# Kernel study: gate matmuls of sample tokens in pairs, state-space outputs of eight heads in one go, and the decays' clamp on ScalarE

## The chip, the cores and the metric

The kernel runs on one NeuronCore of one Trainium2 chip. The metric is the device time of one execution in microseconds. A core has a matrix engine (TensorE, PE in the profile), a vector engine (VectorE, DVE), a scalar engine for activation functions (ScalarE, ACT), a general engine (GpSimd, POOL) and an engine that only issues transfers (SyncE, SP). Each engine has its own list of instructions, in an order set when the program is built; semaphores make one wait for another. Transfers between HBM and SBUF go through queues, here those of SP, ACT and POOL. TensorE's results lie in PSUM, of which the kernel uses eight banks.

## What is computed

One decoder layer for 256 prompt tokens and 8 x 8 sample tokens, 320 columns in all. One input projection feeds two mixers, and their outputs, side by side, go through one output projection; then comes a feed-forward network with a short convolution. The change touches the two mixers. The first gates inside chunks of 128 tokens (16 heads), the second is a state-space scan (SSD, 32 heads in 4 groups):

```python
# chunk_spatial_gate
v = layer_norm(jax.nn.gelu(a_v), ln_g, ln_b)
w = jnp.where(mask[None], w_s[:, :q, :q], 0)
s = jnp.einsum("hts,bnshd->bnthd", w, vp) + b_s
out = jax.nn.gelu(a_u) * s
# ssd_scan
da_cs = jnp.cumsum(dt * a)                       # in a chunk
seg = da_cs[:, :, :, None] - da_cs[:, :, None, :]
decay = jnp.exp(jnp.where(mask, seg, -jnp.inf))
cb = jnp.einsum("bctgn,bcsgn->bctsg", cc, bc)
y_diag = jnp.einsum("bctsgr,bcsgrp->bctgrp", cb[..., None] * decay, xdt)
```

In the kernel the exponent of a decay is clamped at zero before Exp, so that the entries the mask drops stay finite; the mask itself is in `cb`. Weights are float32; each is split into a rounded high part and a low part, and a product of weights and activations is three matmuls (high x high, high x low, low x high).

## The kernel before

**Weights.** `slab` (line 116) loads 128 x 1024 weights through SP's queue, casts them on ScalarE (`whi`, line 128) and subtracts on VectorE (`wlo`, line 130). Each of the three buffers `wraw`, `whi`, `wlo` has three copies. `accumulate` (139) issues the three matmuls, lines 141 to 143, of 320 columns. `project` (166) multiplies into four banks of the pool `mm` and hands each to an evacuation; `chunk_out` (222) multiplies one chunk of mixed activations by `w_out` or `ffn_w_down`. The other four banks, pool `ms`, serve everything small through `misc` (57).

**Order.** The program is unrolled. The framework orders each engine's instructions when the program is built, by priority (by default the place in the program, with `tc.high_priority` and `first` moving things ahead) and by when it estimates that they are ready. `tc.issue_after(x)` puts what is traced inside it, on the engine of `x` only, behind `x` in that engine's order. Background work is written as generators in the list `bg`; `tick` (154) advances the first of them by one step, once or `rate` times behind each slab, and `finish` runs one to its end.

**Gate.** After the v projection `turned` (593) transposes v to tokens on partitions, `vt`, with the prompt's two chunks in columns 0 and 1 of its second axis and the 64 sample tokens on partitions 0 to 63 of column 2; partitions 64 to 127 there are zeroed. `layer_norm` (651) normalizes it in four quarters of 512 features, with rows of gains and offsets that POOL's queue loads, two quarters at once and then one by one as the buffers come free. `gate_mix` (689) does four heads: per head two 128 x 128 matmuls for the prompt (line 710) and one for the samples (711), whose right side `wS` holds the 8 x 8 causal weights as a block diagonal, 64 columns wide. VectorE adds the bias, multiplies by u and splits the result.

**SSD.** `steps` (465) makes the step sizes and the sums of `dt * a`: `nda` holds their negatives with tokens on partitions, and `dacs_d`, in HBM, the sums with tokens along a row. `ssd(g)` (769) is one generator for each group of eight heads: it transposes x, loads states, makes `cb`, and then, for each head, `decays` (876). A pair of heads has one tile `cs` with its rows of sums, broadcast to all partitions by `load_sums` (782; three buffers). For each head `decays` adds the column of `nda` and takes the minimum with 0 (line 889, three pieces: two of 128 columns and one of 64), exponentiates (891) and multiplies by `cb` (893). For a pair it makes `cpx`, the decayed C for the carried state (two buffers). `products(j)` (896) is the matmuls of a pair of heads into one small bank (line 904, float32, half the array's columns a head) and the evacuation on VectorE (914). The generator makes four heads' decays with a step behind each, then two products, then the same again, and loads the fourth pair's sums between.

**Stages.** The SSD generators run behind the slabs of the projections and of `chunk_out` for `w_out`, from about 425 to 730 us. From 810 the post-norm is applied by `x1_ready` (1031) and the FFN begins; `renewals` (1147) holds, at its head, the adds and stores of three prompt states (1158, 1159).

## Time and profile before

| | |
|---|---|
| time, three runs | 1773.45, 1774.44 and 1777.11 us, median 1774.44 |
| the profiled execution | 1774.31 us, its span 1772.6 us |
| granted TensorE clock over the span | 0.999 |
| busiest line of the chain | 141 to 143 on `ps`, 20.7% to 20.9% of the span each |
| float32 matmuls of line 904 | 256 records, 22.0 us busy |
| float32 matmuls of lines 710 and 711 | 64 and 32 records, 15.7 us busy |
| relus and minima | line 889, 96 instructions on VectorE |

The page's first part gives each engine's busy time; the span runs from the first instruction to the last. A matmul in float32 shows as two records, and a matmul's record is its latency: they overlap, so the step from one start to the next, or the pieces of the chain of waits, give what one costs. The chain follows back from the last instruction what released each step. A group's row gives its count, its busy time, the mean of one, then the idle time of the engine in front of it and what ended that.

### The profile page before, as it was taken

Reading aid. Unit: us, or ns where it says so; the run is one execution under the profiler, and the core shown is the slowest. Engines: PE = TensorE matmul, PEld = TensorE weight load, DVE = VectorE, ACT = ScalarE, POOL = GpSimd, SP = SyncE. Lnnn points to the kernel's source line nnn. Section 1 sums busy time; section 2 is a strip of 40 time slices with the busy share of each in tenths; the row PEclk is TensorE's granted clock in tenths of the full one; section 3 lists DMA queues with packets and bytes.
Section 4 is the critical chain, followed back from the end, with each engine's and each line's share of the span. In section 5 each row is a group of like instructions: output and inputs, shape, how many; then the busy total and the mean of one; then the engine's idle time right before and its main releaser. Section 6 shows DMA issues by size and latency. Waiting matters only on the chain.

```text
span 1772.6 us, 31221 instructions
## 1 busy us (share of the span) xinstructions
PE 1765.2 (100%) x12223; PEld 1740.8 (98%) x12223; DVE 1183.2 (67%) x2052; ACT 800.8 (45%) x1111; POOL 281.5 (16%) x593
## 2 busy tenths in 40 slices
PE   9999999999999999999999999999999999999998
PEld 9999999999999999998999999999999999999998
DVE  7448854657877777678866666666666565656475
ACT  7344545333545454445645434343434343433335
POOL 2003210000111111012322212021101010101004
PEclk9999999999999999999999999999999999999999
DMA  7455554445664644444555656566554444444443
GB/s 251 138 167 167 191 156 149 155 152 183 226 208 150 206 154 151 154 164 155 169 190 191 210 177 201 188 196 200 185 187 153 148 155 147 157 148 152 153 148 107
DMA packets 228562, 303.04 MB, mean 171 GB/s; under 512 B 19488, under 2 KB 150656, under 8 KB 228224
## 3 DMA queue, kind: packets, MB, share of 16 engines
q1 hardware_dynamic: 216560, 281.27, 49.6%
q10 hardware_dynamic: 10448, 15.57, 2.4%
q0 software_dynamic: 1408, 4.23, 0.8%
q8 instruction: 96, 1.57, 0.4%
q14 instruction: 50, 0.41, 0.1%
HBM read 283.44 MB, written 17.58 MB: 170 GB/s over the span
## 4 chain that ended last, share of the span: by engine, by line
PE 98%; DVE 1%; DMA 0%; issue 0%; SPq 0%; POOL 0%; ACT 0%; DVEq 0%; ACTq 0%
PE ps L141 21%; PE ps L143 21%; PE ps L142 21%; PE pd L141 10%; PE pd L142 10%; PE pd L143 10%; PE y_ps L904 1%; PE sg L710 0%; PE yo_ps L853 0%; PE up_ps L1198 0%; PE tsum L282 0%; PE xt_ps L382 0%; PE vt_ps L599 0%; DMA vf<-in_w_in 0%; PE s_ps L835 0%; PE x1p L1233 0%
## 5 line engine op out<-in xcount | busy, mean ns | idle before, releaser
L130 DVE TENSOR_TENSOR wlo<-wraw,whi 128x1024 fp32r<-128x1024 f32 x470 | 581.4, 1237 | 383.2 <-ACT whi L128 380.6
L128 ACT CAST whi<-wraw 128x1024 fp32r<-128x1024 f32 x470 | 492.2, 1048 | 703.0 <-PE ps L142 411.5
L141 PE MATMUL ps<-h_hi,whi 128*128 128x320 f32 x2528 | 782.7, 310 | 0.0
L142 PE MATMUL ps<-h_lo,whi 128*128 128x320 f32 x2528 | 780.2, 309 | 1.4 <-DVE h_lo L371 1.4
L143 PE MATMUL ps<-h_hi,wlo 128*128 128x320 f32 x2528 | 779.7, 309 | 0.2 <-DVE wlo L130 0.2
L142 PEld LDWEIGHTS ps<-h_lo,whi 128*128 128x128 f32 x2528 | 475.0, 188 | 2.8 <-DVE h_lo L371 1.9
L141 PEld LDWEIGHTS ps<-h_hi,whi 128*128 128x128 f32 x2528 | 474.7, 188 | 3.1 <-issue 1.6
L143 PEld LDWEIGHTS ps<-h_hi,wlo 128*128 128x128 f32 x2528 | 474.6, 188 | 0.9 <-DVE wlo L130 0.7
L141 PE MATMUL pd<-fhi,whi 128*128 128x320 f32 x704 | 217.3, 309 | 0.0
L143 PE MATMUL pd<-fhi,wlo 128*128 128x320 f32 x704 | 217.3, 309 | 0.0
L142 PE MATMUL pd<-flo,whi 128*128 128x320 f32 x704 | 217.3, 309 | 0.0
L141 PE MATMUL pd<-ohi,whi 128*128 128x320 f32 x448 | 138.7, 310 | 0.0
L142 PE MATMUL pd<-olo,whi 128*128 128x320 f32 x448 | 138.6, 310 | 0.0
L143 PE MATMUL pd<-ohi,wlo 128*128 128x320 f32 x448 | 138.3, 309 | 0.0
L142 PEld LDWEIGHTS pd<-flo,whi 128*128 128x128 f32 x704 | 132.1, 188 | 0.7
L143 PEld LDWEIGHTS pd<-fhi,wlo 128*128 128x128 f32 x704 | 132.1, 188 | 0.0
L141 PEld LDWEIGHTS pd<-fhi,whi 128*128 128x128 f32 x704 | 132.1, 188 | 0.0
L234 DVE TENSOR_TENSOR acc_ffn<-acc_ffn,pd 128x320 f32<-128x320 f32 x160 | 77.3, 483 | 33.2 <-PE pd L143 32.0
L1091 POOL COPY ptf<-pad 128x2 f32<-128x2 f32 x88 | 22.6, 258 | 405.6 <-DVE pad L1079 405.0
L141 PEld LDWEIGHTS pd<-ohi,whi 128*128 128x128 f32 x448 | 84.1, 188 | 0.9 <-issue 0.4
L142 PEld LDWEIGHTS pd<-olo,whi 128*128 128x128 f32 x448 | 84.1, 188 | 0.7 <-issue 0.4
L143 PEld LDWEIGHTS pd<-ohi,wlo 128*128 128x128 f32 x448 | 84.1, 188 | 0.2 <-issue 0.2
(303 smaller groups left out, 1582.6 us busy)
## 6 DMA issues: line engine op xcount, KB each, us to landing
wraw<-in_ffn_w_up SPq DMA_DIRECT2D x176, 512.0 KB, 3.5
wraw<-in_w_in SPq DMA_DIRECT2D x142, 512.0 KB, 3.5
wraw<-in_ffn_w_down SPq DMA_DIRECT2D x88, 512.0 KB, 3.3
wraw<-in_w_out SPq DMA_DIRECT2D x64, 512.0 KB, 3.3
st<-in_state_ssm SPq DMA_DIRECT2D x64, 256.0 KB, 4.6
out_ssm_state_sample<-st ACTq DMA_DIRECT2D x32, 256.0 KB, 2.6
cs<-dacs_d SPq DMA_DIRECT2D x16, 320.0 KB, 4.5
xr<-in_xT SPq DMA_DIRECT2D x4, 640.0 KB, 4.6
```

Of the source, the lines that this page charges most:

```text
L128: act.copy(hi[:, :m], raw[:, :m])
L130: dve.tensor_tensor(out=lo[:, :m], in0=raw[:, :m], in1=hi[:, :m].bitcast(F32), op=ALU.subtract)
L141: pe.matmul(ps, whi, xhi, start=first, stop=False)
L142: pe.matmul(ps, whi, xlo, start=False, stop=False)
L143: newest[0] = pe.matmul(ps, wlo, xhi, start=False, stop=last).ins
L234: dve.tensor_tensor(out=acc[:, nb, :], in0=acc[:, nb, :], in1=ps[:, :NT], op=ALU.add)
L904: pe.matmul(ps[64 * i:64 * i + 64, cols], w(hl), x(hl, m, cpx), tile_position=(0, 64 * i), **flags)
L1091: pool.tensor_copy(ptf[:, k, :], pad[:, 256:258])
```

## The change

- **Paired samples.** The normalized sample rows of the odd heads are copied, quarter by quarter, by four transfers on POOL's queue to partitions 64 to 127 of `vt`'s third column. `wS` becomes two block diagonals side by side for each pair of heads, one on the lower and one on the upper partitions, zero elsewhere, and one matmul of 128 columns makes both heads' samples. `w8` is loaded for 128 partitions.
- **Rows.** The third and fourth quarters' gains and offsets are loaded at once, into buffers of the tag `vf`.
- **Eight heads.** `ssd` makes all eight decays, a step behind each, then a step, then four products. All four `load_sums` come at once; `cs` and `cpx` have four buffers.
- **Clamp.** `sda` holds the sums themselves (copied, not negated). ScalarE takes relu(-m + sda) in three pieces, the column as bias, and then Exp with scale -1; the three VectorE instructions of line 889 go.
- **Order.** The Exp of `cpx` is issued behind the last Silu that stood in the program when the generator began. The prompt states' add and store are traced inside an edge behind the last split of `x1_ready`, which is on ScalarE.
- **Memory.** The descriptor memory of POOL's queue is 1024 bytes a partition instead of 4096.

```diff
...
+        silus = []
+
         def conv_proj(c0, k0, out, soon=0):
...
                 act.activation(o[:, :NP], t[:, :NP], AF.Silu)
-                act.activation(o[:, NP:NT].rearrange("p (b t) -> p b t", b=NB),
-                               t[:, 259:347].rearrange("p (b r) -> p b r", r=11)[:, :, 0:TS], AF.Silu)
+                made = act.activation(o[:, NP:NT].rearrange("p (b t) -> p b t", b=NB),
+                                      t[:, 259:347].rearrange("p (b r) -> p b r", r=11)[:, :, 0:TS], AF.Silu)
+                silus.append(made.ins)
             project(w_in, c0, evac, quiet=4)
...
         dt = op.tile([P, 5, NH], F32, name="dt")
-        nda = op.tile([P, 3, NH], F32, name="nda")
+        sda = op.tile([P, 3, NH], F32, name="sda")
         dec = op.tile([P, 5, NH], F32, name="dec")
...
-            pool.memset(nda[:, 2], 3e38)
+            pool.memset(sda[:, 2], -3e38)
             ps = misc("cs_ps")
...
                 pe.matmul(ps[64 * r:64 * r + 64, 2 * NH:3 * NH], upper_s[:NS], da[:NS, 2], start=True, stop=True, tile_position=(0, 64 * r))
-            dve.tensor_scalar(out=nda[:, 0:2].rearrange("p c h -> p (c h)"), in0=ps[:, :2 * NH], scalar1=-1.0, scalar2=None,
-                              op0=ALU.mult)
-
-            n4 = nda[:, 2].rearrange("p (g r i) -> p g r i", g=4, r=2)
+            dve.tensor_copy(sda[:, 0:2].rearrange("p c h -> p (c h)"), ps[:, :2 * NH])
+
+            n4 = sda[:, 2].rearrange("p (g r i) -> p g r i", g=4, r=2)
             p4 = ps[:, 2 * NH:3 * NH].rearrange("p (g r i) -> p g r i", g=4, r=2)
...
                 x_at, s_at = slice(64 - 64 * r, P - 64 * r), slice(64 * r, 64 * r + 64)
-                dve.tensor_scalar(out=n4[x_at, :, r], in0=p4[x_at, :, r], scalar1=-1.0, scalar2=None, op0=ALU.mult)
+                dve.tensor_copy(n4[x_at, :, r], p4[x_at, :, r])
                 act.activation(ed[s_at], p4[s_at, :, r], AF.Exp)
...
-            wS = gp.tile([P, 4, NB, TS], F32, name="wS")
-            pool.memset(wS[NS:], 0.0)
+            wS = gp.tile([P, 2, 2, NB, TS], F32, name="wS")
+            pool.memset(wS, 0.0)
...
             def turned(g, vf):
-                if g == 0:
-                    pool.memset(vt[NS:, 2], 0.0)
                 for c, (o, n) in enumerate(TOK):
...
-                def load(q):
-                    cs = slice(512 * q, 512 * q + 512)
-                    for name, src in (("lg", gate_ln_g), ("lb", gate_ln_b)):
-                        rows.append(gp.tile([P, 512], F32, tag=name, name=name, bufs=2))
-                        with tc.issue_after(after_v[0]):
-                            pool.dma_start(rows[-1], src[0:1, cs].broadcast_to([P, 512]))
-                load(0)
-                load(1)
+                def load(q, src, row):
+                    with tc.issue_after(after_v[0]):
+                        pool.dma_start(row, src[0:1, 512 * q:512 * q + 512].broadcast_to([P, 512]))
+                    return row
+                both = [("lg", gate_ln_g), ("lb", gate_ln_b)]
+                for q in range(2):
+                    rows.append([load(q, src, gp.tile([P, 512], F32, tag=name, name=name, bufs=2)) for name, src in both])
+                late = [gp.tile([P, 4, NT], F32, tag="vf", name=name, bufs=2).rearrange("p k n -> p (k n)") for name, _ in both]
+                for q in range(2):
+                    rows.append([load(2 + q, src, row[:, 512 * q:512 * q + 512]) for row, (_, src) in zip(late, both)])
                 yield
...
                         v = vt[:n, c, 512 * q:512 * q + 512]
-                        dve.scalar_tensor_tensor(out=v, in0=v, scalar=mv[:n, c, 0:1], in1=rows[2 * q][:n], op0=ALU.subtract, op1=ALU.mult)
-                        dve.scalar_tensor_tensor(out=v, in0=v, scalar=lr[:n, c:c + 1], in1=rows[2 * q + 1][:n], op0=ALU.mult, op1=ALU.add)
-                        if c == 2 and q < 2:
-                            load(q + 2)
+                        dve.scalar_tensor_tensor(out=v, in0=v, scalar=mv[:n, c, 0:1], in1=rows[q][0][:n], op0=ALU.subtract, op1=ALU.mult)
+                        dve.scalar_tensor_tensor(out=v, in0=v, scalar=lr[:n, c:c + 1], in1=rows[q][1][:n], op0=ALU.mult, op1=ALU.add)
+                        if c == 2:
+                            two = vt[:, 2, 512 * q:512 * q + 512].rearrange("p (i r f) -> p i r f", r=2, f=P)
+                            pool.dma_start(two[NS:, :, 0], two[:NS, :, 1])
                         yield
...
                 wT = gp.tile([P, 4, P], F32, tag="wT", name="wT", bufs=1)
-                w8 = gp.tile([NS, 4, TS], F32, tag="w8", name="w8", bufs=1)
+                w8 = gp.tile([P, 4, TS], F32, tag="w8", name="w8", bufs=1)
                 bs = gp.tile([P, 4, P], F32, tag="bs", name="bs", bufs=1)
...
                     for j in range(4):
-                        dve.tensor_tensor(out=wS[:NS, j], in0=w8[:, j].unsqueeze(1).to_broadcast([NS, NB, TS]),
-                                          in1=upper_s[:NS].rearrange("p (b t) -> p b t", b=NB), op=ALU.mult)
+                        rs = slice(NS * (j % 2), NS * (j % 2) + NS)
+                        dve.tensor_tensor(out=wS[rs, j // 2, j % 2], in0=w8[rs, j].unsqueeze(1).to_broadcast([NS, NB, TS]),
+                                          in1=upper_s[rs].rearrange("p (b t) -> p b t", b=NB), op=ALU.mult)
                 yield
...
                         pe.matmul(ps[:, P * c:P * c + P], vt[:, c, fs], wT[:, j, :], start=True, stop=True)
-                    pe.matmul(ps[:, NP:NT], vt[:, 2, fs], wS[:, j].rearrange("p b t -> p (b t)"), start=True, stop=True)
+                    if j % 2 == 0:
+                        pe.matmul(ps[:, NP:NP + 2 * NS], vt[:, 2, fs], wS[:, j // 2].rearrange("p r b t -> p (r b t)"), start=True, stop=True)
+                        of_two = ps[:, NP:NP + 2 * NS].rearrange("p (r b t) -> p r b t", r=2, b=NB)
                     s = tp.tile([P, NT], F32, tag="ev", name="s", bufs=2)
...
                     dve.tensor_tensor(out=s[:, NP:].rearrange("p (b t) -> p b t", b=NB),
-                                      in0=ps[:, NP:NT].rearrange("p (b t) -> p b t", b=NB),
+                                      in0=of_two[:, j % 2],
                                       in1=bs[:, j, :TS].unsqueeze(1).to_broadcast([P, NB, TS]), op=ALU.add)
...
-                xs = x_of[g]
+                xs, last_silu = x_of[g], silus[-1]
                 h0 = 8 * g
...
-                    cs = sd.tile([P, 2, NT], F32, tag="cs", name="cs", bufs=3)
+                    cs = sd.tile([P, 2, NT], F32, tag="cs", name="cs", bufs=4)
                     o = NS * (j // 2)
...
                 yield from repeat(None, 5)
-                sums_of = {j: load_sums(j) for j in range(3)}
+                sums_of = {j: load_sums(j) for j in range(4)}
                 yield
...
                         cs = sums_of.pop(j)
-                        cpx = sd.tile([P, 2, P], F32, tag="cpx", name="cpx", bufs=2)
-                        act.activation(cpx, cs[:, :, at[1][0]:at[1][0] + P], AF.Exp)
+                        cpx = sd.tile([P, 2, P], F32, tag="cpx", name="cpx", bufs=4)
+                        with tc.issue_after(last_silu):
+                            act.activation(cpx, cs[:, :, at[1][0]:at[1][0] + P], AF.Exp)
                         pool.tensor_tensor(out=cpx, in0=cpx, in1=cT[:, g, P:2 * P].unsqueeze(1).to_broadcast([P, 2, P]),
...
                     for c, (o, n) in enumerate(at):
-                        dve.tensor_scalar(out=m[:, o:o + n], in0=m[:, o:o + n], scalar1=nda[:, c, h0 + hl:h0 + hl + 1],
-                                          scalar2=0.0, op0=ALU.add, op1=ALU.min)
-                    act.activation(m, m, AF.Exp)
+                        act.activation(m[:, o:o + n], m[:, o:o + n], AF.Relu, bias=sda[:, c, h0 + hl:h0 + hl + 1], scale=-1.0)
+                    act.activation(m, m, AF.Exp, scale=-1.0)
                     o = NS * (hl // 4)
...
                 x1d = decayed(1, 1)
-                for j in range(0, 4, 2):
-                    for hl in range(2 * j, 2 * j + 4):
-                        decays(hl)
-                        yield
+                for hl in range(8):
+                    decays(hl)
                     yield
+                yield
+                for j in range(4):
                     products(j)
-                    products(j + 1)
-                    if j == 0:
-                        sums_of[3] = load_sums(3)
                 pool.tensor_tensor(out=by_head(s1), in0=by_head(s1),
...
                 yield
-                pool.tensor_tensor(out=s1, in0=s1, in1=x1d, op=ALU.add)
-                act.dma_start(o_ssm_p[g], s1)
+                with tc.issue_after(whole[KD - 1]):
+                    pool.tensor_tensor(out=s1, in0=s1, in1=x1d, op=ALU.add)
+                    act.dma_start(o_ssm_p[g], s1)
...
         "gate_wT": w_s.transpose(2, 0, 1),
-        "gate_w8": np.concatenate([w8] * NB),
+        "gate_w8": np.concatenate([w8] * (P // TS)),
         "gate_b_s": a["gate_b_s"], "ssm_dt_bias": a["ssm_dt_bias"], "ssm_a_log": a["ssm_a_log"],
...
-    nc = _bacc.Bacc("TRN2", target_bir_lowering=False, num_devices=1, dynamic_dma_scratch_size=4096)
+    nc = _bacc.Bacc("TRN2", target_bir_lowering=False, num_devices=1, dynamic_dma_scratch_size=1024)
     arrays = laid_out({k: _np.asarray(v) for k, v in inputs.items()})
...
```

## The prediction

> **What bounds the kernel now.** I read the page first: span, busy shares, the chain of waits.
>
> ```profile
> span 1772.6 us, 31221 instructions
> PE 1765.2 (100%) x12223; PEld 1740.8 (98%) x12223; DVE 1183.2 (67%) x2052; ACT 800.8 (45%) x1111; POOL 281.5 (16%) x593
> PE 98%; DVE 1%; DMA 0%; issue 0%; SPq 0%; POOL 0%; ACT 0%; DVEq 0%; ACTq 0%
> ```
>
> TensorE is busy for 1765.2 of 1772.6 us and makes 98% of the chain that ended last. The other four engines have room over the whole span, but a share over the span says nothing of a stage, so I took the stages in which the diff does something (start:end, length, then busy time of PE, PEld, DVE, ACT, POOL, the granted clock, DMA share, GB/s), then TensorE's own waits (us in all, times, longest) and, in the timeline of ScalarE, the last Silu of the fourth group and two weight casts that follow each other.
>
> ```profile
> 145.00:260.00 115.00, 115.00 (x791) 114.02 (x789) 85.10 (x162) 59.51 (x85) 30.92 (x54) 1.00 0.56 174
> 515.00:730.00 215.00, 214.76 (x1620) 206.73 (x1613) 160.69 (x323) 107.94 (x157) 24.11 (x43) 1.00 0.52 168
> 676.00:705.00 29.00, 28.76 (x246) 26.13 (x246) 22.39 (x44) 12.16 (x18) 4.69 (x4) 1.00 0.45 141
> 810.00:822.00 12.00, 10.63 (x51) 7.32 (x50) 9.44 (x20) 6.04 (x11) 4.00 (x3) 0.86 0.30 108
> PE ps L142 <- DVE h_lo L371: 1.4, 2, 1.2
> 676.21 0.25 ACT L427 ACTIVATE xs<-cv 128x64 f32<-128x64 f32 x1
> ...
> 687.85 1.05 ACT L128 CAST whi<-wraw 128x1024 fp32r<-128x1024 f32 x1 [2.47 <-PE pd L142]
> 691.37 1.05 ACT L128 CAST whi<-wraw 128x1024 fp32r<-128x1024 f32 x1 [2.47 <-PE pd L142]
> ```
>
> In the layer-norm stage (145 to 260) and in the SSD stage (from 425; its last 215 us are the second row) TensorE has no idle time worth the name: 0.24 us in 330. The casts are 691.37 - 687.85 = 3.52 us apart, one weight slab; a slab is 8 blocks of three matmuls, so a weight matmul takes TensorE 0.147. An edit there can shorten the run only where it takes work off TensorE, and can lengthen it only where it makes TensorE wait. VectorE, at 75% of that second row, and ScalarE, at 50%, are not what ends last there. The one place with a wait that the diff comes near is 810:822, where TensorE stands 1.4 us for the first parts of the FFN's input.
>
> **The paired samples (lines 710 and 711).** The chain of waits around one group's gate matmuls, TensorE from one weight slab to the next; xN counts records, two for a float32 matmul:
>
> ```profile
> 259.52 0.44 PE sg L710 x4
> 259.96 0.17 PE sg L711 x2
> 260.13 0.50 PE sg L710 x4
> ...
> 262.14 0.20 PE ps L141
> ...
> 434.15 0.87 PE xt_ps L382 x8
> ```
>
> Four heads take 262.14 - 259.52 = 2.62 us. A record with 128 columns costs 0.44 / 4 = 0.11; one with 64 columns costs 0.17 / 2 = 0.085, not half, and the next four then cost 0.50 instead of 0.44, so a 64-column matmul hides the next weight load badly. After the change each pair of heads has one 128-column matmul where it had two of 64: four heads have 16 + 4 = 20 records of 128 columns. The transposes (eight in 0.87, 0.109 each) say that such a record holds its price in a row. 20 x 0.11 = 2.20, so 0.42 is saved for each of four groups: **1.7 us**, all on the path. From below: if the paired matmul cost as much as the two it replaces (0.34), only the 0.06 behind two of them would go, 0.1 in a group, 0.4 in all. I take 1.7, since the records of the same shape stand right beside it.
>
> ```profile
> L669 POOL DMA_DIRECT2D lb<-in_gate_ln_b x4 | 2.2, 541 | 0.4 <-DVE vt L677 0.4
> ...
> L130 DVE TENSOR_TENSOR wlo<-wraw,whi 128x1024 fp32r<-128x1024 f32 x470 | 581.4, 1237 | 383.2 <-ACT whi L128 380.6
> ...
> L914 DVE SCALAR_TENSOR_TENSOR xs<-xs,prm,y_ps 128x320 f32<-128x320 f32 x16 | 8.6, 542 | 7.9 <-PE y_ps L904 7.9
> ```
>
> What this edit needs lies off the path: four more transfers on POOL's queue (odd heads' rows copied to partitions 64 to 127, each issued behind the last normalization step of its quarter), the same small VectorE products on other partitions, a larger w8. On POOL's queue the conv stage's padding copies stand behind those transfers, VectorE's evacuation behind the copies, and TensorE's next use of those banks behind the evacuation; the row 145:260 shows 84 us of idle POOL and 30 of idle VectorE in that stretch. I cost it at nothing; without that cover the four issues, at 0.541 each as line 669's, would come to 2.2 us. (The other two rows of this view of groups are for the banks, below.) The same holds for the layer-norm rows, now loaded at once into buffers of the v projections: the loads no longer stand behind VectorE's steps, and the steps they feed end long before the matmuls at 259.52.
>
> **The y products in one go (line 904).** Chain rows, first group and then the second:
>
> ```profile
> 478.25 1.69 PE y_ps L904 x32
> 479.94 0.35 PE pd L141
> ...
> 559.27 0.36 PE y_ps L904 x2
> 559.63 0.34 PE pd L142
> ...
> 560.41 1.69 PE y_ps L904 x27
> ...
> 576.22 0.36 PE y_ps L904 x2
> ...
> 577.08 0.91 PE y_ps L904 x13
> ...
> 581.27 0.36 PE y_ps L904 x2
> ...
> 582.00 0.92 PE y_ps L904 x13
> ```
>
> A block of two products takes 1.69, and the first weight matmul behind it 0.35 where one takes 0.147: each return from float32 to the split weights costs 0.20. One block a group instead of two saves one return in the first, third and fourth group: 0.6 us. The second group is cut up today: its pieces add up to 0.36 + 1.69 + 0.36 + 0.91 + 0.36 + 0.92 = 4.60 where two blocks would be 3.38, and weight matmuls stand behind four of the pieces, the first at 0.34, where one block has one return. Whole, it saves 1.22 + 0.6. So the term lies between 0.6, if the new order is cut up as much as the old, and 2.4. The order of each engine is fixed when the program is built, and no row shows the new one. All eight heads' decays now stand well ahead of the first product, with buffers for all of them (cs 4, cpx 4), which speaks for whole blocks; ScalarE has more to do before them, which speaks for pieces. I take the middle, **1.5 us**.
>
> **The clamp moved to ScalarE (lines 889 and 891).** Groups by line and form, count, then busy time and mean ns:
>
> ```profile
> L891 ACT ACTIVATE cs<-cs 128x320 f32<-128x320 f32 x32 | 14.3, 466 | 20.3 <-DVE cs L889 20.1
> L367 ACT CAST ohi<-s 128x320 fp32r<-128x320 f32 x16 | 7.3, 459 | 16.5 <-DVE s L719 16.4
> L882 ACT ACTIVATE cpx<-cs 128x256 f32<-128x256 f32 x16 | 6.7, 416 | 11.4 <-DMA cs<-dacs_d 11.1 <-PE y_ps L904 0.2
> L370 ACT ACTIVATE ohi<-xs,prm 128x320 fp32r<-128x320 f32 x12 | 6.3, 556 | 0.0
> L427 ACT ACTIVATE xs<-cv 128x64 f32<-128x64 f32 x16 | 3.9, 242 | 0.0
> L891 ACT ACT_TABLE_LOAD x3 | 3.8, 1283 | 0.1
> ...
> L889 DVE TENSOR_SCALAR cs<-cs,nda 128x128 f32<-128x128 f32 x64 | 19.7, 335 | 6.0 <-DMA cs<-dacs_d 5.2 <-ACT cpx L882 0.7
> L889 DVE TENSOR_SCALAR cs<-cs,nda 128x64 f32<-128x64 f32 x32 | 8.4, 264 | 0.0
> ```
>
> VectorE is rid of 19.7 + 8.4 = 28.1 us. ScalarE gets 64 relus of 128 columns and 32 of 64, which no row shows. Without a per-partition operand 64 columns take 242 and 256 take 416, so 128 lie at 300; such an operand costs 556 - 459 = 97. That gives 397 and 339: 25.4 + 10.8 = 36.2 us, or 27.0 if the bias were free. I take 36.2, since the bias here is a column as the scale of line 370 is.
>
> A head then costs ScalarE 2 x 0.397 + 0.339 + 0.466 = 1.60 us, a group of eight with four of line 882 14.5 us. Two heads beside one slab's cast: 3.20 + 0.42 + 1.05 = 4.67, where a slab takes TensorE 3.52. So ScalarE falls 1.15 us behind with each slab of decays, 4.6 over four. What hides it: the casts of the slabs stand ahead by priority and wait 2.47 us for a free buffer before each, with three buffers (two slabs, 7.0 us, less 1.05 for the cast and 1.24 for the subtraction behind it); and the decays need not run beside the slabs of their ticks. They wait only for their sums, a buffer and the last Silu. The tightest group is the fourth, whose last Silu starts at 676.21: in 676:705 ScalarE has 12.16 us now, decays of its first heads among them; with all of these kept, 12.16 + 14.5 = 26.7 of 29. It fits, so I cost it at **nothing**. From above, with that cover gone, the products wait 4.6 us in each group, 18.4 in all. From below there is no gain, since VectorE is off the path.
>
> A table load takes 1.283 us; if relu and Exp did not share a table, each head would add two. The Trainium skill (ScalarE: Activation LUTs, "Table sets: the hidden batching unit") says that relu is in every set; by it no load is added, and otherwise the 64 loads would be an estimated 82 us of ScalarE. No run here shows it yet. The edge behind the last Silu also keeps Exp from falling between Silus, so loads go rather than come; ScalarE's time alone.
>
> **Edits with no cost of their own.** Four loads of sums instead of three and one: the same transfers on SP's queue, none now stuck between slabs behind a product. The larger memset of wS, the smaller descriptor memory and the dropped memset of vt are POOL's, at 16% of the span. Four y banks are taken at once where two were: a rival below. The adds and stores of the three prompt states (lines 1158, 1159):
>
> ```profile
> 820.68 1.02 ACT L370 ACTIVATE h_hi<-acc_mix,prm 128x320 fp32r<-128x320 f32 x2 [2.34 <-DVE acc_mix L1037]
> ```
>
> The edge holds back only what is queued on the engine of its anchor, ScalarE: the stores move behind the last split, POOL's adds do not. The split at 820.68 waited for VectorE, not for the stores, so I take 0; at most the 1.4 us of waits there go.
>
> **The sum.** 1.7 + 1.5 = 3.2 us off the profiled execution of 1774.31 (span 1772.6 and 1.7 around it), which lies 0.13 below the median of 1774.44: **1771.1 us**.
>
> **Rivals.** (1) More goes: the y blocks come out whole and the states' edge clears the gap at 818. 1774.31 - 1.7 - 2.4 - 1.4 = 1768.8. For it: the pieces of today's second group; against: POOL's adds stay beside VectorE's steps, which are what TensorE waits for there. (2) Part is given back at the banks: products 3 and 4 need two more of the four small banks, and where one is still held TensorE waits for VectorE's evacuation behind one subtraction, 1.24 + 0.54 = 1.8 us a time; in two groups 3.6, so 1774.7. Against it: a block lasts 3.4 us, and evacuation follows within. (3) **Slower:** ScalarE becomes what TensorE waits for. The order was fixed with the products where the decays should be done; if ScalarE is 4.6 us late in the third and fourth group, whose decays all lie behind a late Silu, that is 9.2: 1780.3. It turns the sign when the waits exceed 3.2 us in all, and is over 0.2% from 6.7. For it: 4.67 against 3.52 a slab; against: ScalarE idles 16.8 of 29 us in its tightest window today. The Trainium skill (ScalarE: Activation LUTs, "Rules for kernel authors") speaks for this rival: relu and min belong on VectorE. Our rows bear it out in engine time only, 28.1 us there against an estimated 36.2 here.
>
> **Chances.** Forecast 0.47 (own range 1769.9 to 1772.2, two fifths of it under 1770.9), rival 1 0.19, rival 2 0.14, rival 3 0.18, the rest a wait on POOL's queue. With 0.2% (3.5 us, about what a measurement of this kernel can tell from no change) around 1774.44: faster 0.39, same 0.40, slower 0.21. The range 1769.0 to 1778.5 leaves out most of rival 3 and the lower edge of rival 1.
>
> **What would show it.** Sixteen records of line 711 instead of 32, and a gate block of 2.20 us: right on the pairs. Line 904 in four blocks of about 3.4 us: 2.4 rather than 1.5. Relus near 397 and 339 ns, no more table loads than now, and no row in which TensorE waits for the products' VectorE step or for whi: the clamp is hidden. Any such wait above 1 us a group, and the forecast falls towards rival 3.

## The result and the profile after

| | before | changed |
|---|---|---|
| median of 8 executions each, us | 1773.59 | 1769.62 |
| lowest and highest | 1773.27, 1777.11 | 1769.41, 1770.74 |
| profiled execution | 1774.31, span 1772.6 | 1769.41, span 1767.7 |

The ratio is 0.9973, with a 95% interval of 0.9964 to 0.9982: faster by 0.27%, 4.0 us between the medians, where 3.2 were forecast. (The two profiled executions lie 4.9 apart: that of before is 0.7 above its median, that of the changed kernel 0.2 below.) Two executions of the runs below, at granted clocks of 0.79 and 0.56, took 3178 and 2878 us; no median, difference or ratio counts them. The page of the changed kernel, its first part (busy time of each engine) and the shares of its chain of waits:

```profile
span 1767.7 us, 31184 instructions
PE 1758.7 (99%) x12207; PEld 1737.5 (98%) x12207; DVE 1163.9 (66%) x1956; ACT 815.9 (46%) x1201; POOL 266.5 (15%) x596
PE 98%; DVE 1%; DMA 0%; ACT 0%; issue 0%; POOL 0%; DVEq 0%; ACTq 0%
```

TensorE bounds it as before, with 6.5 us less of busy time. **Where the time went** is read by putting rows of the two chains side by side that stand for the same instructions. First before, then after (start, length, engine, what):

```profile
133.92 1.31 PE vt_ps L599 x12
205.99 1.03 PE dt_ps L470 x10
464.06 0.86 PE s_ps L835 x2
541.08 0.56 PE tsum L282 x6
641.60 0.56 PE tsum L282 x6
730.46 0.56 PE tsum L282 x6
1757.37 0.65 PE x1p L1233 x2
```

```profile
133.54 1.31 PE vt_ps L599 x12
205.25 1.03 PE dt_ps L473 x10
461.55 0.86 PE s_ps L841 x2
538.23 0.56 PE tsum L282 x6
637.49 0.56 PE tsum L282 x6
725.98 0.56 PE tsum L282 x6
1752.48 0.65 PE x1p L1237 x2
```

The lead grows from 0.38 to 0.74 (the layer norm's stage), 2.51 (the gate blocks, 206 to 464), 2.85, 4.11 and 4.48 (the four groups' y) and 4.89. The first 0.38 and the last 0.41 of it lie where the two kernels do the same work and other kernels scatter as much. The chain around the first gate block and two of the y blocks:

```profile
258.77 0.44 PE sg L714 x4
259.22 0.22 PE sg L716 x2
259.44 0.89 PE sg L714 x8
260.33 0.22 PE sg L716 x2
260.56 0.45 PE sg L714 x4
261.00 0.15 PE ps L141
...
482.78 3.23 PE y_ps L910 x64
...
605.90 3.24 PE y_ps L910 x64
```

A gate block takes 261.00 - 258.77 = 2.23 us, and the weight matmul behind it 0.15 where it took 0.20. The y blocks are whole in all four groups: four pairs of heads in 3.23, less than two of the old blocks (3.38). The first weight matmul behind a y block still takes 0.34, but behind the gate block, which is float32 too, 0.15: the return that the prediction priced at 0.20 goes with the y matmuls, which use half the array's columns, and not with float32 as such. Of ScalarE, groups by line and form:

```profile
L896 ACT ACTIVATE cs<-cs,sda 128x128 f32<-128x128 f32 x64 | 23.8, 391 | 5.7 <-DMA cs<-dacs_d 5.7
L896 ACT ACTIVATE cs<-cs,sda 128x64 f32<-128x64 f32 x32 | 10.7, 335 | 0.0
L428 ACT ACT_TABLE_LOAD x4 | 5.1, 1283 | 0.1
L889 ACT ACT_TABLE_LOAD x4 | 5.1, 1283 | 0.1
```

The relus take 391 and 335 ns (forecast 397 and 339), 34.5 us in all. The Trainium skill (ScalarE: Activation LUTs, "What ACT_TABLE_LOAD costs") gives 280 ns and 0.833 a column for an activation with a column as bias, an estimate of 387 and 333; the trace agrees, and that was nearer than the forecast's sum. With Silu, cpx and decays 9 table loads (4, 4 and 1 for the decays' Exp) are left of 14, and none stands at the relus' line. TensorE's new wait in these stages (us, times, longest; the 1.4 us behind line 371 are as before, and 0.5 behind line 370, new here, shows in before with the pairs too), and ScalarE's timeline there:

```profile
PE xt_ps L382 <- ACT xs L428: 1.2, 1, 1.2
```

```profile
568.74 1.17 ACT L896 ACTIVATE cs<-cs,sda 128x128 f32<-128x128 f32 x4 [1.43 <-DMA cs<-dacs_d]
569.82 0.40 ACT L428 ACTIVATE xs<-cv 128x256 f32<-128x256 f32 x1
570.12 0.24 ACT L429 ACTIVATE xs<-cv 128x64 f32<-128x64 f32 x1
570.38 1.28 ACT L889 ACT_TABLE_LOAD   x1
```

Four relus stand ahead of the third group's last Silu and wait there 1.43 us for the sums; TensorE's transposes of x wait for that Silu. The edge on cpx holds the table load behind the Silus (570.38), but nothing holds the relus.

### The profile page after: what moved, and what is told of

It reads as the page before. It is cut to its first block, busy times and chain, and to the rows that moved or that the text cites. A ratio compares the mean times of both kernels' runs of the same rounds, so it can differ in the third digit from the quotient of the medians.

```text
span 1767.7 us, 31184 instructions
## 1 busy us (share of the span) xinstructions
PE 1758.7 (99%) x12207; PEld 1737.5 (98%) x12207; DVE 1163.9 (66%) x1956; ACT 815.9 (46%) x1201; POOL 266.5 (15%) x596
## 4 chain that ended last, share of the span: by engine, by line
PE 98%; DVE 1%; DMA 0%; ACT 0%; issue 0%; POOL 0%; DVEq 0%; ACTq 0%
PE ps L141 21%; PE ps L143 21%; PE ps L142 21%; PE pd L141 10%; PE pd L143 10%; PE pd L142 10%; PE y_ps L910 1%; PE yo_ps L859 0%; PE up_ps L1202 0%; PE sg L714 0%; PE tsum L282 0%; PE xt_ps L382 0%; PE vt_ps L599 0%; PE early L70 0%; PE s_ps L841 0%; DMA cs<-dacs_d 0%
```

## The experiments

Each row gives the median against the median of before in the same runs, and the ratio with its interval. "Changed" is the changed kernel, with one thing undone or added; "before" is the kernel before, with one thing done.

| kernel | us against before | ratio, 95% interval |
|---|---|---|
| changed, once more | -4.55 | 0.9975, 0.9966 to 0.9984 |
| changed, clamp on VectorE | -2.26 | 0.9987, 0.9978 to 0.9996 |
| changed, that and sums asked for early | -2.43 | 0.9983, 0.9974 to 0.9992 |
| changed, short stand on VectorE | -3.55 | 0.9980, 0.9971 to 0.9988 |
| changed, additions on VectorE as well | +1.40 | 1.0008, 0.9999 to 1.0017 |
| changed, four heads at a time | -2.08 | 0.9988, 0.9980 to 0.9997 |
| changed, rows late | -2.34 | 0.9988, 0.9979 to 0.9997 |
| changed, no edge on cpx | -3.90 | 0.9979, 0.9970 to 0.9988 |
| changed, no edge on the states | -3.82 | 0.9979, 0.9970 to 0.9988 |
| changed, relus held | -5.25 | 0.9971, 0.9960 to 0.9983 |
| changed, relus held, once more | -5.36 | 0.9971, 0.9958 to 0.9983 |
| changed, relus held, sums early | -5.50 | 0.9969, 0.9958 to 0.9981 |
| before, pairs | -1.77 | 0.9991, 0.9982 to 0.9999 |
| before, clamp on ScalarE | +0.33 | 1.0002, 0.9993 to 1.0011 |
| before, eight heads | +1.77 | 1.0010, 1.0002 to 1.0019 |
| before, early rows | -1.55 | 0.9991, 0.9982 to 1.0000 |
| before, small descriptor memory | +0.46 | 1.0001, 0.9992 to 1.0009 |

The traces tell in which stage a change acts, which the medians do not. These are the lengths of the stages against before, us, from the same rows of the chain as above (starts near 134, 206, 464, 541, 642, 730, the end):

| kernel | to 206 | to 464 | to 541 | to 642 | to 730 | to the end |
|---|---|---|---|---|---|---|
| changed | -0.36 | -1.77 | -0.34 | -1.26 | -0.37 | -0.41 |
| changed, once more | -0.36 | -1.85 | -0.34 | -0.91 | -0.37 | -0.61 |
| clamp on VectorE | -0.35 | -0.67 | +0.92 | -2.21 | -0.38 | +0.19 |
| clamp on VectorE, sums early | -0.36 | +1.32 | +0.16 | -2.21 | -0.36 | -0.04 |
| short stand | -0.36 | -1.85 | -0.34 | -0.68 | -0.39 | -0.43 |
| four heads | -0.36 | -1.60 | 0.00 | +1.26 | -0.03 | +0.41 |
| rows late | +1.42 | -1.84 | -0.34 | -0.96 | -0.38 | -0.57 |
| no edge on cpx | -0.35 | -1.86 | -0.34 | -0.54 | -0.34 | -0.29 |
| no edge on the states | -0.36 | -1.86 | -0.33 | -0.88 | -0.39 | +0.45 |
| relus held | -0.36 | -1.85 | -0.34 | -2.21 | -0.39 | -0.06 |
| relus held, once more | -0.36 | -1.85 | -0.34 | -2.20 | -0.37 | -0.20 |
| relus held, sums early | -0.35 | -1.84 | -0.36 | -2.21 | -0.37 | +0.56 |
| before, pairs | +0.39 | -1.85 | 0.00 | 0.00 | +0.01 | -0.58 |
| before, clamp | -0.36 | 0.00 | 0.00 | +0.81 | +0.01 | -0.65 |
| before, eight heads | +1.45 | +2.19 | +0.41 | +1.96 | -0.96 | +0.43 |
| before, early rows | -0.36 | +0.11 | +0.01 | +0.76 | +0.01 | -0.45 |
| before, small memory | +2.54 | +0.20 | +0.02 | +0.63 | +0.05 | -0.60 |

Two columns hold scatter of their own: before with early rows and before with the small memory do the same as before between 541 and 642 and took 0.8 and 0.6 longer there, and from 730 on, where most kernels are alike, the values lie anywhere from -0.65 to +0.56.

**The clamp back on VectorE.**

```diff
-                        act.activation(m[:, o:o + n], m[:, o:o + n], AF.Relu, bias=sda[...], scale=-1.0)
-                    act.activation(m, m, AF.Exp, scale=-1.0)
+                        dve.tensor_scalar(out=m[:, o:o + n], in0=m[:, o:o + n], scalar1=nda[...], scalar2=0.0, op0=ALU.add, op1=ALU.min)
+                    act.activation(m, m, AF.Exp)
```

> The changed kernel with the clamp put back on VectorE (sums negated, add and minimum there, Exp with scale +1), all else as changed. Theory: the clamp on ScalarE brings nothing and costs the one new wait of TensorE, 1.16 us for the Silus of the third group's x behind the relus; without it the y blocks stay whole at 3.24 us, that wait goes, and the time is 1768.2 to 1768.8 us, 0.8 to 1.4 under the changed kernel's 1769.62. Rival: the 28.1 us taken off VectorE are what lets all eight heads' decays be done in time; then the y blocks are cut up again or wait for VectorE, and the time is 1770.5 to 1772 us.

The theory fell: the kernel is 1.7 to 2.3 us slower than the changed one. One half of it was right (541 to 642: -2.21, the wait for the Silu down to 0.2), but 2.4 are lost in the two stages ahead of it: -0.67 for -1.85, and +0.92 for -0.34. The chain of that kernel in the first group:

```profile
449.15 0.80 DVE cs L897 x4
449.95 1.13 DVE wlo L130
...
453.12 1.23 DVE wlo L130
454.37 0.42 DVE pad L416
```

VectorE's 24 additions stand in its order ahead of subtractions and of the evacuation (`pad`) that frees TensorE's banks; the chain leaves TensorE and runs along them. In the second of these stages it comes to the additions by way of the sums' transfer:

```profile
485.12 5.15 DMA cs<-dacs_d
...
490.50 0.25 DVE cs L897
```

**Parts alone on the kernel before**: the clamp; the eight heads (with the smaller descriptor memory, which they need); the pairs.

> The kernel before with the clamp alone moved to ScalarE. Theory: nothing gained, and at most one wait like the 1.16 us of the changed kernel, perhaps more than one since four heads' decays must now be ready at a time; 1773.4 to 1775.0 us against 1773.59. Rival: it is worth something by itself (VectorE's evacuations sooner, y less cut up): 1771.5 to 1772.8 us.

> The kernel before with the eight heads alone (four buffers of cs and cpx, all sums at once, four products together; less descriptor memory for POOL so that it fits), clamp on VectorE, no edges. Theory: y comes in four blocks of 3.24 us, worth 2.4 (1.2 of it in the second group): 1771.0 to 1771.5 us. Rival: the y blocks are whole only because the clamp left VectorE; then they are cut up and the gain is at most 0.6: 1773.0 to 1773.6 us.

> The kernel before with the paired samples alone. Theory: a gate block of 2.23 us for 2.62 in each of four groups, 1.6 in all: 1771.9 to 1772.1 us. Rival: part of that is given back, because the transfers of the odd heads' rows stand on POOL's queue among the loads of the rows of gains and offsets: 1772.6 to 1773.6 us.

The clamp alone does nothing, as the theory had it. The eight heads alone are slower, which neither the theory nor its rival had: 2.19 us more up to 464, where its chain too runs along the additions, and the third group's transposes wait 1.9 us for the Silu. Some of its loss is the late rows' (+1.45), and its trace overstates the rest: the profiled execution was the slowest of its eleven, 3.6 us above their median. The pairs bring 1.85 in the trace and 1.77 in the median.

**Stand or length.** Three runs ask what on VectorE costs this: that it stands for the sums' transfer with evacuations queued behind, or the length of the additions. The first asks for the sums five steps earlier; the second puts the stand alone into the changed kernel, a copy of two columns that nothing uses; the third the additions alone, on data that is always there.

```diff
-                yield from repeat(None, 5)
                 sums_of = {j: load_sums(j) for j in range(4)}
-                yield
+                yield from repeat(None, 6)
...
+                        dve.tensor_copy(junk, cs[:, :, NT - 1])
                         cpx = sd.tile([P, 2, P], F32, tag="cpx", name="cpx", bufs=4)
...
+                        dve.tensor_scalar(out=junk[:, :n], in0=ident[:, :n], scalar1=sda[...], scalar2=0.0, op0=ALU.add, op1=ALU.min)
                     act.activation(m, m, AF.Exp, scale=-1.0)
```

> The changed kernel with the clamp on VectorE and the four loads of sums five steps earlier; TensorE's and VectorE's orders are those of the kernel with the clamp on VectorE, which stood 2.3 us under before. Theory: what that kernel lost against the changed one (1.7 us) is VectorE standing in its order for the sums (DMA, 1.70 us in the first group, with evacuations queued behind) and TensorE behind it; with the sums there, 3.3 to 4.2 us under before and no wait of TensorE for pad or acc_mix above 0.3. Rival: it is the length of 24 additions, some 8 us of VectorE, in front of the evacuations, wherever the sums are: still 1.8 to 2.8 us under before, and the waits for pad remain.

> The changed kernel, clamp on ScalarE, with one copy of 2 columns on VectorE for each pair's sums, which nothing uses: it stands in VectorE's order where the clamp's additions stand in the kernel with the clamp on VectorE, and waits for the same transfer, but is short. The changed kernel is 4.4 to 4.8 us under before, the one with the clamp on VectorE 2.3. Theory: it is VectorE's stand for the sums (1.70 and 2.11 us in the first two groups there) that delays the evacuations behind it: 2.0 to 3.2 us under before, with a wait of TensorE for pad or acc_mix. Rival: the length of the additions: 3.9 to 4.8 us under before.

> The changed kernel, clamp on ScalarE, with VectorE doing the 96 additions and minima beside it on data that is there all the time, into a tile that nothing reads: the length of the clamp on VectorE without its wait for the sums. Theory: without the wait the additions fill VectorE's idle time and cost at most 0.8: 3.6 to 4.8 us under before. Rival: the length is what the evacuations wait for: 2.0 to 3.2 us under before.

The first run's median falls to the rival, but it didn't make what it was to test. Counted from its row near 206, VectorE's sums were asked for 230.00 us later in the first group, where the kernel without the edit asked for them after 229.98, and took 9.82 us to land; from the second group on the loads wait for their buffers, which the products of the group before hold. The chain of the changed kernel shows that too:

```profile
564.03 0.94 PE y_ps L910 x16
...
564.99 3.67 DMA cs<-dacs_d
```

Since the sums landed at other times, the run still tells something. These are the first additions of the first two groups with VectorE's stand for the sums, in the kernel with the clamp on VectorE and then in this one:

```profile
443.38 2.05 DVE L897 TENSOR_SCALAR cs<-cs,nda 128x128 f32<-128x128 f32 x8 [1.70 <-DMA cs<-dacs_d]
490.30 0.45 DVE L897 TENSOR_SCALAR cs<-cs,nda 128x128 f32<-128x128 f32 x2 [2.11 <-DMA cs<-dacs_d]
```

```profile
445.88 2.05 DVE L896 TENSOR_SCALAR cs<-cs,nda 128x128 f32<-128x128 f32 x8 [3.68 <-DMA cs<-dacs_d]
492.04 0.45 DVE L896 TENSOR_SCALAR cs<-cs,nda 128x128 f32<-128x128 f32 x2 [1.37 <-DMA cs<-dacs_d]
```

In the first group the stand is 1.98 us longer and the stage 1.99 (+1.32 for -0.67); in the second it is 0.74 shorter and the stage 0.76 (+0.16 for +0.92). With 24 additions behind it, the stand is paid in full in both groups.

The other two runs take the halves apart. The second of VectorE's waits in the short stand's kernel from 430 to 740 (us, times, longest), TensorE's longest in the kernel with the additions beside, and the view of their tile there (durations, first and last start):

```profile
DVE junk L888 <- DMA cs<-dacs_d: 13.3, 11, 2.8
```

```profile
PE fin_ps L939 <- DVE xs L923: 3.1, 1, 3.1
```

```profile
L898 DVE TENSOR_SCALAR junk<-ident,sda x94: 241/285/1032, 430.1 to 525.0; 128x128 f32<-128x128 f32 x62, 128x64 f32<-128x64 f32 x32
```

VectorE stands 13.3 us for the sums, and up to 541 TensorE loses none of it: -1.85 and -0.34 as in the changed kernel. (The median, -3.55, lies between theory and rival; the trace's one difference is a longer wait for the Silu, 1.7 us, in the stage to 642.) With the additions it loses 5.2 us between 206 and 541. That is more than the clamp's 2.4, since with no sums to wait for nearly all of four groups' additions ran in these 95 us; the size is not the clamp's, the direction is. So a stand alone costs nothing, and what the clamp on VectorE costs is a stand and a burst of additions one behind the other, ahead of the evacuations. What 24 additions a group would cost with the sums there in time, no run shows.

**Four heads at a time, the clamp on ScalarE** (`cs` with three buffers, `cpx` with two, the old loop).

> The changed kernel with the decays and products made four heads and two pairs at a time again (three buffers of cs, two of cpx), the clamp on ScalarE. Theory: y in pieces again costs 2.4 us, less 1.1 for the wait of TensorE for the Silus if it goes with it: 1.6 to 2.8 us under before. Rival: the pieces cost nothing net, as the blocks of the eight heads alone gained nothing: 3.6 to 4.2 us under before.

As the theory had it: 1.9 to 2.5 us are lost, in the stages where y is cut up again (0.00 for -0.34, +1.26 for -1.26, -0.03 for -0.37). Not all of the +1.26 is pieces: TensorE waits 0.9 us for VectorE there (0.6 behind line 361, 0.3 behind line 899).

**Rows and descriptor memory.** Three runs: the rows late in the changed kernel, the smaller memory alone in before, and the rows early alone in before (the first edit below the other way round).

```diff
-                late = [gp.tile([P, 4, NT], F32, tag="vf", ...) ...]
+                        if c == 2 and q < 2:
+                            load(q + 2)
...
-    nc = _bacc.Bacc("TRN2", ..., dynamic_dma_scratch_size=4096)
+    nc = _bacc.Bacc("TRN2", ..., dynamic_dma_scratch_size=1024)
```

> The changed kernel with the third and fourth quarters' gains and offsets loaded one by one again. Theory: with the smaller descriptor memory POOL issues these loads later, VectorE stands some 5 us for the offsets (3.1 to 3.8 in kernels with the larger memory, 5.1 in the one with eight heads alone), and TensorE, with casts and subtractions ahead for some 3 us only, waits 1.5 us for wlo between 165 and 190: 2.2 to 2.8 us under before. Rival: the late rows cost TensorE 0.36 at most whatever the memory: 3.6 to 4.0 us under before.

> The kernel before with the smaller descriptor memory of POOL's queue alone. Theory: POOL issues the late rows later, VectorE stands some 5 us for the offsets (3.8 before) and TensorE loses 1.4 us more between 165 and 190: 1.0 to 1.8 us above before. Rival: the memory does nothing and the loss seen with eight heads came from the scatter of that stage: within 0.4 us of before.

> The kernel before with the rows of gains and offsets loaded early alone, the descriptor memory as before. Theory: VectorE's stand of 3 to 3.8 us for the offsets goes, and TensorE's 0 to 0.75 behind it: 0.2 to 0.6 us under before. Rival: the transfers at once delay the weights' slabs, and nothing or less is left: 0.2 us under to 0.5 above before.

VectorE's first step with the third quarter's offsets in the timeline of before, with TensorE's weight load that waits for a slab's subtraction behind it, and in its chain TensorE's long pieces (0.37 and 0.27 for 0.147); then, in the timeline of before with the small memory, the same step and TensorE's wait:

```profile
175.53 0.75 DVE L677 SCALAR_TENSOR_TENSOR vt<-vt,rs_r,lb 128x512 f32<-128x512 f32 x1 [3.81 <-DMA lb<-in_gate_ln_b]
...
181.25 0.19 PEld L143 LDWEIGHTS ps<-h_hi,wlo 128*128 128x128 f32 x1 [0.22 <-DVE wlo L130]
```

```profile
181.29 0.37 PE ps L143
187.38 0.27 PE ps L141
```

```profile
178.28 0.75 DVE L677 SCALAR_TENSOR_TENSOR vt<-vt,rs_r,lb 128x512 f32<-128x512 f32 x1 [5.13 <-DMA lb<-in_gate_ln_b]
...
180.22 0.42 PE L143 MATMUL ps<-h_hi,wlo 128*128 128x320 f32 x1 [1.55 <-DVE wlo L130]
```

With late rows this stage is 0.36 shorter to 2.54 us longer than in the profiled execution of before, from one kernel to the next; with early rows it is -0.35 or -0.36 in all of them. Early rows alone bring 1.55 us in the median, more than theory and rival, with an interval that touches no change, and narrow the executions: 1773.14 to 1774.70 in eleven, where before took 1773.26 to 1777.88 in 33 beside them. That all of the 1.55 comes from this stage is not shown. Late rows in the changed kernel cost 1.6 to 2.2, in the theory's range, though VectorE's stand there was 3.95 us and not 5. Whether the smaller memory makes late rows worse is open: its profiled execution, the slowest of its eleven, lost 2.54, its median 0.46, which fits neither expectation. All three kernels with late rows and the small memory lost 1.4 us or more in this stage (+1.42, +1.45, +2.54), and the three with the large memory did not (-0.36, 0, +0.39); that speaks for it and is no proof, one profile each.

**The two edges** (their `issue_after` lines taken away).

> The changed kernel without the edge that holds the Exp of cpx behind the last Silu. Theory: Exp falls among the Silus again, with table loads between (more than the changed kernel's 17), and the Silus that TensorE's transposes of x wait for come later, as in the kernel with eight heads alone (a wait of 1.9 us): 2.0 to 3.2 us under before. Rival: the edge does nothing on the path: 3.8 to 4.2 us under before.

> The changed kernel with the prompt states' adds and stores where they were, without their edge. Theory: the 0.4 to 0.6 us that the changed kernel's trace gains between 810 and 865 over that of before are a dip of the granted clock to 0.91 in the profiled execution of before, not the edge, which brings nothing or costs 0.2: 4.0 to 4.3 us under before. Rival: the edge brings that gain: 3.4 to 3.6 us under before.

Without the edge on cpx, ScalarE's timeline shows the mechanism of the theory at the same place, a load to Exp and one back ahead of the last Silu:

```profile
569.60 1.28 ACT L888 ACT_TABLE_LOAD   x1 [2.26 <-DMA cs<-dacs_d]
570.89 0.42 ACT L888 ACTIVATE cpx<-cs 128x256 f32<-128x256 f32 x1
571.33 1.28 ACT L428 ACT_TABLE_LOAD   x1
572.62 0.42 ACT L428 ACTIVATE xs<-cv 128x256 f32<-128x256 f32 x1
```

But the relus already cost most of that wait with the edge, so -0.54 stands for -0.91 to -1.26, and the median falls to the rival. Without the edge on the states the median lies between the two expectations, and the trace shows nothing beyond the scatter of the last column; the clock of 0.86 that before had in 810:822 is 1.00 in the changed kernel and 0.86 again without the edge, but 0.86 too in the changed kernel with its rows late, which has the edge.

**The relus held too**, and with the sums asked for early; the changed kernel ran beside them.

```diff
                     for c, (o, n) in enumerate(at):
-                        act.activation(m[:, o:o + n], ..., AF.Relu, ...)
+                        with tc.issue_after(last_silu):
+                            act.activation(m[:, o:o + n], ..., AF.Relu, ...)
```

> The changed kernel with its relus also issued behind the last Silu, as the Exp of cpx is. The changed kernel stands 4.0 us under the one before; all times here are against the kernel before in the same runs. Theory: TensorE's one new wait (1.16 us, for the Silus of x that stand behind the relus of the second group's last heads) goes: 4.7 to 5.3 us under before, and the view of waits has no row for xt_ps. Rival: the relus, held, come too late for the products, and TensorE waits for the decays or VectorE's products instead: 2.0 to 4.0 us under before.

> The changed kernel once more, beside the two below. Theory: 4.0 to 5.0 us under before in these runs too, with little scatter (some 1.3 us), and TensorE's wait for the Silus of x of 1.2 to 1.5 us again in its trace, as it comes from the order of ScalarE's instructions. Rival: that wait was of one execution, and is not there now; or the lead over before belongs to the first runs and is now under 3.5 us.

> The changed kernel with the relus behind the last Silu, beside the changed kernel on the same chip. Theory: without the wait of 1.2 to 1.5 us it is 0.6 to 1.3 us under the changed kernel's median in these runs. Rival: the wait is paid for anyway (other waits of TensorE take it up): within 0.3 us of the changed kernel.

> The changed kernel with the relus behind the last Silu and the loads of sums five steps earlier. Theory: relus stand some microseconds for the sums in the changed kernel (1.43 in the third group) with casts queued behind them, which are hidden by the casts' lead, so that it is within 0.3 us of the kernel with the held relus. Rival: earlier sums let ScalarE finish sooner, and TensorE gains another 0.3 us or more.

ScalarE's timeline with the held relus, where the Silu waits for its own input alone:

```profile
569.33 0.42 ACT L428 ACTIVATE xs<-cv 128x256 f32<-128x256 f32 x1 [1.39 <-DVE cv L423]
```

The wait was there again in the changed kernel (1.5 us). With the relus held 0.2 of it are left, the stage to 642 is at -2.20 or -2.21 each time, 0.95 and 1.3 better, and the median 1769.38 beside 1770.19 on the same chip: 0.8 us, as the theory had it. Early sums change it by 0.14, within the expectation's 0.3. The held relus make the fastest kernel of this study, by less than the intervals of the ratios can show; the stage and the missing wait show it.

## Where the prediction was right, and which step failed

The forecast of 1771.1 lies 1.5 above the measured 1769.62. Half of that is no error of the sum: it started from 1774.31, and eight executions put the kernel before at 1773.59. The other half, 0.8, is the sum. At 3.2 us it stayed just inside 0.2%, so that "within 0.2%" got the largest chance; the kernel is 0.27% faster. What failed is the size of three terms: y, taken at 1.5, brought 2.9; the rows, put at nothing, brought 0.36 or more; and the clamp, put at nothing, cost 0.95 to 1.3 in one wait. That the last offsets part of the first two is luck.

- **Pairs, 1.7:** right. The block is 2.23 (2.20 forecast), the saving 1.77 to 1.85 in the traces with what the matmul behind it saves, 1.77 in the median of the part alone.
- **y, 1.5, the middle of 0.6 to 2.4:** the step that failed first. All blocks are whole, and with the relus held the three stages give 0.34 + 2.21 + 0.39 = 2.9 us. The rows that spoke for pieces (a fuller ScalarE) did not decide it; TensorE's order was fixed with four whole blocks. That 2.9 lies above even the upper bound is the price of a whole block: the working took it at two old ones, 2 x 1.69 = 3.38, and it takes 3.23, which is 0.15 a group and 0.6 in all, 2.4 + 0.6 = 3.0. In the first group, 0.15 and one return of 0.20 make 0.35, and the stage gives 0.34.
- **Rows, 0:** failed too, in its reason. The prediction said that these steps "end long before the matmuls at 259.52", which was the wrong reader to look at: VectorE, standing 3.81 us for the offsets, is late with the subtraction of a weight slab, and TensorE waits for that one. Nor could the row 145:260 show it, where TensorE is busy for all of 115.00 us: a matmul's record overlaps the next, and a short wait shows only as a longer step in the chain. The gain is 0.36 in the profiled execution; the 1.55 in the median of early rows alone is not shown to be all of this stage. The idle POOL and VectorE of that stage hid nothing, because the stand stood in the order ahead of `wlo`.
- **Clamp, nothing:** right for the clamp alone (+0.33, interval on both sides of no change), wrong as a reason. "VectorE is off the path" holds over a stage, not in the 9 us in which 24 additions, behind a stand for their sums, come ahead of an evacuation. Beside the eight heads the move is worth 1.7 to 2.3 us, and without it they bring next to nothing (2.26 in all, of which the pairs alone bring 1.77); its own cost is the wait of the slower rival. The Trainium skill's rule (ScalarE: Activation LUTs, "Rules for kernel authors") that relu and min belong on VectorE is right in engine time (28.1 us there, 34.5 here). For the kernel the measurement says otherwise: nothing clear with the clamp moved alone, 1.7 to 2.3 us in ScalarE's favour beside the eight heads.
- **The slower rival** had its mechanism right and its place wrong: ScalarE came late once, by 1.2 to 1.5 us, at the Silu and not at the products, in the third group, and not in the fourth. Its cover for the casts held.
- **Banks (rival 2):** no wait of that kind is in the trace.
- **Table loads, the states' edge, 0:** right on the loads (9 for 14, no wait), and no run shows anything of the edge beyond the scatter from 730 on.

The sum was 3.2. With what the runs show it is 0.36 + 1.8 + 2.9 - 1.1 = 4.0 us in the profiled stages, beside 4.0 and 4.5 in the two medians. With the 1.55 of early rows alone in place of the 0.36 it would be 5.2, more than either median, so parts measured alone need not add up.

## What to carry to other kernels

Ask of an engine that is off the path not how busy it is, but what stands in its order ahead of the few instructions that the bounding engine waits for: 24 additions in a burst, behind a stand for the transfer that feeds them, cost 2.4 us in two groups; the same additions for four heads at a time cost nothing that shows, and 13.3 us of stands without them nothing either. Parts of one change can be worth more together than alone, so cost the pair: with the pairs and the early rows in each, the eight heads without the clamp's move come to 2.3 us, the move without the eight heads to 2.1, and both together to 4.0 to 4.5. An edge that keeps one operation behind a deadline has to hold every operation that is fed by the same late transfer.

## What the runs showed that was not expected

The granted clock dipped in one window of some profiled executions and not of others whose work there is the same: from 810 to 822 it was 0.86 in eight of the 19 profiles, that of before among them, and 1.00 in the others. The time from 730 to the end does not follow it: -0.60 to +0.56 with the dip, -0.65 to +0.43 without. What brings it on stays open.

From 730 on, kernels whose order there is the same differ by up to 1.2 us from one profile to the next, so half a microsecond between two single profiles says nothing of a change. And a load whose wait leaves TensorE free in one execution (3.05 us of VectorE's time for the offsets in before with the clamp moved, no loss) costs 1.55 us in another, at 5.13: a wait near the end of what hides it shows as scatter of the median rather than as a row of the profile.
